# First FFN product: left operands begun three steps ahead instead of two, a ring of four, and weight blocks loaded in the order of use

## The chip, the cores and the metric

The kernel runs on one core of one Trainium2 chip. The core has five engines that work at the same time, each through its own list of instructions in the order in which the program issued them: TensorE (PE in the profile; PEld is its weight load), VectorE (DVE), ScalarE (ACT), GpSimd (POOL) and SyncE (SP), which here only issues transfers between DRAM and on-chip memory. An instruction that needs another engine's result or a transfer waits, and everything behind it in its list waits too. The metric is the device time of one execution in microseconds, lower is better.

## What is computed

An encoder trunk of two layers over x of 1024 tokens by 1024 features: layer 0 is a gated linear attention, layer 1 a chunked softmax attention, and each is followed by the same kind of convolutional FFN. The change lies in the FFN:

```python
D_MODEL = 1024; SEQ = 1024; DEPTH = 2; FFN_DIM = 2816; FFN_CONV = 3

def conv_ffn(xn, w_up, conv_w, conv_b, w_down):
    h = causal_dwconv(xn @ w_up, conv_w) + conv_b      # w_up: 1024 x 5632
    gate, val = h[..., :FFN_DIM], h[..., FFN_DIM:]
    return (jax.nn.silu(gate) * val) @ w_down          # w_down: 2816 x 1024

for layer in range(DEPTH):
    ...
    h = h + conv_ffn(rmsnorm(h, f_norm[layer]), f_w_up[layer], f_conv[layer], f_conv_b[layer], f_w_down[layer])
return rmsnorm(h, final_norm)
```

## The kernel before

**Precision.** Each float32 factor is cut in two numbers of the type fp32r, a high part (a copy on ACT, `cut_high`, L1370) and a low part (source minus high part, mostly on POOL, `cut_low`, L1375, shown in the profile under the helper's line L1355). A product is then three matmuls: high by high, high by low, low by high (`triple`, L1384 to L1386). In the profile the left operand of the first product is `uh` and `ul`, that of the second product `dh` and `dl`, and the raw weights behind them are `r` and `dr`.

**Columns and products.** The FFN's 5632 hidden columns are 22 column pairs j, each one block of 128 gate columns and one of 128 val columns. For one pair, the weights are four raw blocks (11, 12, 21, 22; upper and lower half of the features, gate and val), each loaded by SP with 256 KB (`load`, L1427). Column 0 takes eight plain products. For every other pair the 2 x 2 blocks are multiplied in the manner of Strassen and Winograd with seven products n, in the order 1, 7, 6, 5, 2, 4, 3. Each is one step of twelve matmuls of 512 columns, 2.7 us. The left operand of a product is built by `operand(j, n)` (L1433): for n = 7, 6, 5 and 3 a sum of raw blocks in place on DVE (`r<-r,r`), then the cast `uh` on ACT, then the subtraction `ul` on POOL. The first few products (those before (1, 3)) take the low part on DVE, and are begun two steps ahead. The right operands X are sums of the input halves, built once.

**After a product.** `after(j, n)` (L1495) runs in the step behind product n and adds the accumulator into `keep`, `vpre` or `gpre`. When a column's seven products are done, its conv runs: three taps of val and of gate (the first on ACT, L1464, two more on DVE, L1467), silu on ACT (L1470), the product with val on DVE, and the cut of the hidden block (`hidh` on ACT, L1482, `hidl` on DVE).

**The second product** (`down(g, u)`, L1660) runs in between: nine groups g of two columns, eight output tiles u = d0 to d7 each. From column 3 on, a period of two columns runs on PE as n3' d0 | n1 n7 d1 n6 d2 n5 n2 d3 n4 d4 n3 | n1' d5 n7' d6 n6' n5' d7 n2' n4' n3' d0, where n and n' are products of the odd and the even column; the first two groups of layer 0 and the first of layer 1 are woven in at other places. For even u the operand dr is loaded five steps ahead and cut two steps ahead of its use (dh on ACT, dl on POOL); it serves two tiles. The running sum of a tile over the groups lies in DRAM: `load_h` fetches it to one of two tiles `hr`, `down_sum` (L1684, the step behind the product) adds the new part on DVE (`hr<-pd,hr`) and SP writes it back.

**The order.** All of it is written out by hand. `seq` is the list of PE's steps, and `jobs` holds for each step what the other engines begin in it, with a rank. The loop issues the jobs of step i in the order of their ranks, those of the same rank in the order in which they were entered, and then the step itself:

```python
for i in range(len(seq) + 8):
    for _, f in sorted(jobs.pop(i, ()), key=lambda j_: j_[0]):
        f()
    if i < len(seq):
        seq[i]()
```

Ranks that matter: 0 for `after` and `down_sum`, 1 for the left operands of the first product and, entered later, for the cut of dr, about 2 for the conv, 3 for loads of weights, 5 for `load_h`. So in one step DVE sees first the sums of the step behind, then the `r` sums, then the conv. Tiles come from rings: a tag with `bufs` tiles, where a new tile waits until the oldest is free. `uh` and `ul` have rings of three, of which `tmp()` (L1792) lends tiles to the norm behind the FFN; r11, r21 and r22 have two tiles each, r12 one. `pos[j, s]` with s from 1 to 7 is the step of the s-th product of column j in the order above, so s = 2 is product 7 and s = 3 is product 6.

## Time and profile before

| | us |
|---|---|
| median of 3 runs | 2670.28 (2663.6 to 2670.86) |
| the profiled execution | 2677.71 |
| its span in the trace | 2676.0 |

The mean granted clock of PE in the profiled execution is 0.993 of full speed. In the rows of the profile a group reads: line, engine, operation, result<-sources, shape, count, then busy time and mean length of one in ns, then the idle time ahead of them on their engine and what ended it. In a timeline each row is start, length, engine, line, operation, and in brackets the idle time before it with what ended it. In the list of waits: who waited for whom, the total in us, how many times, and the longest. Matmul records overlap, so the distance between starts is their pace, not their length. The lines that carry the argument stand in the prediction.

### The profile page before, as it was taken

What the parts mean: (1) busy time and instruction counts of PE and PEld (TensorE: products, weight loads), DVE (VectorE), ACT (ScalarE), POOL (GpSimd) and SP (SyncE); (2) the same over time, 40 slices, a digit from 0 to 9 for tenths busy, and PEclk for the clock granted to TensorE, in tenths of its full rate; (3) what the DMA queues carried; (4) which work ended last, traced back from release to release, by engine and by line L of the source; (5) the groups of instructions that cost most, each with busy time, mean ns of one, the idle gap of its engine ahead of it and who ended that gap; (6) DMA issues with size and microseconds to landing.
All of it is one profiled execution on the core that took longest, in us unless ns stands there. A gap on an engine that the chain in (4) does not pass through costs nothing.

```text
span 2676.0 us, 40971 instructions
## 1 busy us (share of the span) xinstructions
PE 2577.5 (96%) x15013; PEld 2160.6 (81%) x15013; DVE 1656.1 (62%) x2968; ACT 1190.8 (44%) x2398; POOL 1136.6 (42%) x1202
## 2 busy tenths in 40 slices
PE   7999999999999999999999999998999999999998
PEld 5888788888777778888778888887777888888886
DVE  5756765554765556666775666666487565655667
ACT  5444546563443333333455555555354333333333
POOL 3655543346343343443435444434343343343441
PEclk9999999999999999999999999999999999999999
DMA  4534345456245555555531111114222555565554
GB/s 131 135 102 117 116 121 158 140 166 180 66 134 191 189 192 185 189 189 192 189 110 50 49 51 47 42 48 147 88 87 87 174 192 190 194 204 189 189 177 146
DMA packets 335065, 370.86 MB, mean 139 GB/s; under 512 B 34576, under 2 KB 256528, under 8 KB 334864
## 3 DMA queue, kind: packets, MB, share of 16 engines
q1 hardware_dynamic: 329328, 357.50, 42.3%
q10 hardware_dynamic: 4896, 8.65, 0.9%
q0 software_dynamic: 640, 2.10, 0.3%
q8 instruction: 118, 1.93, 0.3%
q14 instruction: 83, 0.68, 0.1%
HBM read 250.15 MB, written 118.03 MB: 138 GB/s over the span
## 4 chain that ended last, share of the span: by engine, by line
PE 56%; issue 13%; POOL 8%; DVE 7%; DMA 4%; ACT 1%; SPq 1%; POOLq 0%; DVEq 0%; ACTq 0%
PE pu L1386 6%; PE pu L1385 6%; PE pu L1384 6%; POOL ul L1355 5%; PE acc L120 4%; PE acc L121 4%; PE acc L122 4%; PE pd L1682 2%; PE pd L1681 2%; PE pd L1680 2%; PE acco L120 2%; PE acco L122 2%; PE acco L121 2%; PE ptp L1999 2%; DMA dr<-in_f_w_down_dram 2%
## 5 line engine op out<-in xcount | busy, mean ns | idle before, releaser
L1355 POOL TENSOR_TENSOR ul<-r,uh 128x512 fp32r<-128x512 f32 x282 | 402.3, 1435 | 669.4 <-ACT uh L1372 651.3
L1372 ACT CAST uh<-r 128x512 fp32r<-128x512 f32 x296 | 177.7, 618 | 536.8 <-DVE r L1355 499.9
L1355 DVE TENSOR_TENSOR hr<-pd,hr 128x1024 f32<-128x1024 f32 x136 | 166.4, 1223 | 352.9 <-DMA hr<-d_hu 192.7
L120 PE MATMUL acc<-xh,whi 128*128 128x512 f32 x896 | 375.8, 420 | 0.2 <-ACT xh L1094 0.2
L121 PE MATMUL acc<-xl,whi 128*128 128x512 f32 x896 | 354.4, 396 | 1.6 <-POOL xl L379 0.9
L122 PE MATMUL acc<-xh,wlo 128*128 128x512 f32 x896 | 353.3, 394 | 0.5 <-POOL wlo L105 0.5
L105 POOL TENSOR_TENSOR wlo<-wraw,whi 128x256 fp32r<-128x256 f32 (+1 forms) x293 | 235.9, 834 | 200.1 <-ACT whi L103 159.3
L1386 PE MATMUL pu<-xh,ul 128*128 128x512 f32 x552 | 217.4, 394 | 10.6 <-POOL ul L1355 10.4
L1384 PE MATMUL pu<-xh,uh 128*128 128x512 f32 x552 | 216.2, 392 | 1.7 <-DVE h L1256 0.9
L1385 PE MATMUL pu<-xl,uh 128*128 128x512 f32 x552 | 215.6, 391 | 1.0 <-POOL xl L379 1.0
L122 PEld LDWEIGHTS acc<-xh,wlo 128*128 128x128 f32 x896 | 169.3, 189 | 38.4 <-POOL wlo L105 1.0
L121 PEld LDWEIGHTS acc<-xl,whi 128*128 128x128 f32 x896 | 170.5, 190 | 25.9 <-POOL xl L379 3.1
L120 PEld LDWEIGHTS acc<-xh,whi 128*128 128x128 f32 x896 | 170.2, 190 | 23.2 <-ACT xh L1094 1.1
L1680 PE MATMUL pd<-dh,hidh 128*128 128x256 f32 x576 | 163.3, 284 | 0.0
L1682 PE MATMUL pd<-dh,hidl 128*128 128x256 f32 x576 | 163.0, 283 | 0.0
L1681 PE MATMUL pd<-dl,hidh 128*128 128x256 f32 x576 | 163.0, 283 | 0.0
L1467 DVE SCALAR_TENSOR_TENSOR val<-vpre,colt,val 128x1023 f32<-128x1023 f32 (+2 forms) x92 | 127.9, 1390 | 40.1 <-ACT val L1464 39.9
L1979 POOL TENSOR_SCALAR sS<-sS,st 128x640 f32<-128x640 f32 (+4 forms) x128 | 88.1, 691 | 144.9 <-DVE st L1978 121.4
L1355 POOL TENSOR_TENSOR dl<-dr,dh 128x512 fp32r<-128x512 f32 x72 | 98.7, 1371 | 105.8 <-ACT dh L1372 103.9
L1355 DVE TENSOR_TENSOR r<-r,r 128x512 f32<-128x512 f32 x168 | 136.2, 811 | 4.8 <-POOL ul L1355 4.7
L1386 PEld LDWEIGHTS pu<-xh,ul 128*128 128x128 f32 x552 | 103.6, 188 | 41.0 <-POOL ul L1355 19.6
L1977 ACT ACTIVATE sS<-sS,st 128x640 f32<-128x640 f32 (+4 forms) x128 | 89.2, 697 | 82.6 <-DVE st L1976 79.9
(374 smaller groups left out, 6738.2 us busy)
## 6 DMA issues: line engine op xcount, KB each, us to landing
d_hu<-hr SPq DMA_DIRECT2D x144, 512.0 KB, 3.0
hr<-d_hu SPq DMA_DIRECT2D x128, 512.0 KB, 5.0
r<-in_f_w_up_dram SPq DMA_DIRECT2D x168, 256.0 KB, 4.4
dr<-in_f_w_down_dram SPq DMA_DIRECT2D x72, 256.0 KB, 4.7
wraw<-in_a_w_in_dram SPq DMA_DIRECT2D x32, 512.0 KB, 4.6
wraw<-in_a_w_out_dram SPq DMA_DIRECT2D x16, 512.0 KB, 4.3
d_r<-h ACTq DMA_DIRECT2D x32, 256.0 KB, 4.0
wraw<-in_w_kv_dram SPq DMA_DIRECT2D x16, 512.0 KB, 4.0
```

What stands on the lines that cost most here:

```text
L105: nc.gpsimd.tensor_tensor(lo[:, c], raw[:, c], hi[:, c].bitcast(F32), op=ALU.subtract)
L120: mm(ps, hi[:, kw, wcol : wcol + P], rh[k][s], start=st, stop=False)
L121: mm(ps, hi[:, kw, wcol : wcol + P], rl[k][s], start=False, stop=False)
L122: mm(ps, lo[:, kw, wcol : wcol + P], rh[k][s], start=False, stop=sp)
L1355: tt = lambda eng, o, a, b, op: eng.tensor_tensor(o, a, b, op=op)
L1372: copy(hi, src)
L1384: mm(ps, w[0][:, cw], x[0], start=first, stop=False, skip_group_check=True)
L1385: mm(ps, w[0][:, cw], x[1], start=False, stop=False, skip_group_check=True)
L1386: mm(ps, w[1][:, cw], x[0], start=False, stop=last, skip_group_check=True)
L1680: mm(o_, hh, w_[0][:, c], start=i == 0 and g != u, stop=False, skip_group_check=True)
L1681: mm(o_, hh, w_[1][:, c], start=False, stop=False, skip_group_check=True)
L1682: mm(o_, hl, w_[0][:, c], start=False, stop=i == 1, skip_group_check=True)
```

## The change

Left operands from product (1, 3) on are issued three steps ahead of their product in place of two, at the same rank. The rings of `uh` and `ul` get a fourth tile, in both places where their size is given. The loads of the next column's blocks 11 and 21 change places, so that 11 (used by products 1, then 5) is asked for at product 7 of the column before and 21 (first used by product 7) at product 6. The cut of dr, the conv, the sums and the order of PE's steps are left as they are.

```diff
         def cut_high(src, ring, copy=nc.scalar.copy):
-            hi, lo = [wf.tile([P, HALF], F32R, name=ring + x, tag=ring + x, bufs=3 if ring == "u" else 2) for x in "hl"]
+            hi, lo = [wf.tile([P, HALF], F32R, name=ring + x, tag=ring + x, bufs=4 if ring == "u" else 2) for x in "hl"]
             copy(hi, src)
             return hi, lo
...
             else:
-                at(i - 2, lambda j=j, n=n: operand(j, n), 1)
+                at(i - 3, lambda j=j, n=n: operand(j, n), 1)
             if n != 2 or j > 2:
                 at(i + 1, lambda j=j, n=n: after(j, n), 0)
...
         for j in range(3, FP - 1):
-            for q, s in ((21, 2), (11, 3), (22, 4), (12, 7)):
+            for q, s in ((11, 2), (21, 3), (22, 4), (12, 7)):
                 at(pos[j, s], lambda j=j, q=q: load(j + 1, q), 3)
...
                 def tmp():
                     rooms.append(rooms.pop(0))
-                    return wf.tile([P, HALF], F32, name="nt", tag=rooms[-1], bufs=3)
+                    return wf.tile([P, HALF], F32, name="nt", tag=rooms[-1], bufs=4)
```

## The prediction

> **What bounds the kernel now.** I read the head of the page first, then the waits of TensorE (PE), over the span and stretch by stretch, then the timeline of each engine around single waits.

> ```profile
> span 2676.0 us, 40971 instructions
> PE 2577.5 (96%) x15013; PEld 2160.6 (81%) x15013; DVE 1656.1 (62%) x2968; ACT 1190.8 (44%) x2398; POOL 1136.6 (42%) x1202
> L1355 DVE TENSOR_TENSOR hr<-pd,hr 128x1024 f32<-128x1024 f32 x136 | 166.4, 1223 | 352.9 <-DMA hr<-d_hu 192.7
> ```

> PE is busy for 96% of the span and its matmuls stay the same in number and order. So the change can only shorten PE's waits in the two FFN stretches (some 680 to 1326 us and 1990 to 2626 us), or add to them. The third row is needed below: the running sum of the second product (hr) waits 192.7 us for its own reload from DRAM, and what stands behind such a sum in VectorE's (DVE's) order waits with it. The waits of PE, first the whole span, then 716 to 750, 750 to 875, 875 to 1300, 1300 to 1326, 2000 to 2040, 2135 to 2596 and 2596 to 2626 us (total, times, longest):

> ```profile
> PE pu L1386 <- POOL ul L1355: 19.6, 24, 1.7
> ...
> PE pu L1386 <- POOL ul L1355: 2.3, 2, 1.7
> PE pu L1384 <- DVE keep L1355: 1.1, 1, 1.1
> ...
> PE pu L1386 <- POOL ul L1355: 2.8, 4, 0.9
> PE pu L1384 <- ACT uh L1372: 1.2, 2, 0.9
> ...
> PE pu L1386 <- POOL ul L1355: 4.8, 7, 1.0
> ...
> PE pu L1384 <- ACT uh L1372: 0.4, 1, 0.4
> ...
> PE pu L1386 <- POOL ul L1355: 1.5, 2, 0.9
> ...
> PE pu L1386 <- POOL ul L1355: 2.3, 2, 1.7
> ...
> PE pu L1386 <- POOL ul L1355: 1.4, 2, 1.2
> ...
> PE pu L1386 <- POOL ul L1355: 1.8, 3, 0.8
> PE pu L1384 <- ACT uh L1372: 1.3, 1, 1.3
> ```

> These are the waits for the left operands, uh and ul. 16.9 of the first row's 19.6 us are found again in the stretches: that is what there is to win, about 1% with all that hangs on it. One such wait, on ScalarE (ACT), GpSimd (POOL) and PE:

> ```profile
> 1172.12 1.06 ACT L1470 ACTIVATE gate<-gate 128x1024 f32<-128x1024 f32 x1 [5.77 <-DVE gate L1467]
> 1173.09 1.12 ACT L1372 CAST uh<-r 128x512 fp32r<-128x512 f32 x2
> ...
> 1173.77 3.10 POOL L1355 TENSOR_TENSOR ul<-r,uh 128x512 fp32r<-128x512 f32 x2 [6.05 <-ACT uh L1372]
> ...
> 1174.31 0.39 PE L1385 MATMUL pu<-xl,uh 128*128 128x512 f32 x1
> 1175.67 0.50 PE L1386 MATMUL pu<-xh,ul 128*128 128x512 f32 x1 [0.97 <-POOL ul L1355]
> ```

> The cast of operand (j,2) stands behind silu on ACT, and silu had waited 5.77 us for DVE. A matmul starts 0.227 us after the one before it where nothing waits (two in 0.45 us, from 1224.35 to 1224.80 below). Here 1.36 us pass: 1.13 us are lost for a wait that reads 0.97, so each wait costs its figure plus 0.16.

> **What the change removes.** The cast and the low part go one step (2.7 us, twelve matmuls) earlier. In this example they come ahead of silu, and the wait goes. From 875 to 1300 us that saves 4.8 + 0.4 + 8 x 0.16 = 6.5 us, from 2135 to 2596 us 1.4 + 2 x 0.16 = 1.7 us: **-8.2**. At the end of layer 0 it is 1.5 + 0.3 = 1.8, of which I take -1.5. At the end of layer 1 it is 1.8 + 1.3 + 4 x 0.16 = 3.7 and one stretch at half clock:

> ```profile
> 2613.60:2617.00 3.40, 1.72 (x7) 0.78 (x5) 2.48 (x4) 2.09 (x3) 1.09 (x1) 1.00 0.02 5
> 2617.10:2620.40 3.30, 3.16 (x8) 2.49 (x9) 2.96 (x4) 0.25 (x1) 0.08 (x1) 0.50 0.27 79
> ...
> 737.00:740.40 3.40, 2.52 (x11) 2.13 (x12) 2.17 (x2) 1.45 (x3) 3.40 (x3) 1.00 0.26 106
> ```

> (Columns: stretch, its length, PE, PEld, DVE, ACT, POOL busy, granted clock, DMA share, GB/s.) In the first row PE is idle for 1.68 us of 3.40, and the next stretch runs at 0.50: 8 matmuls where 3.30 / 0.227 = 14.5 fit, so 1.5 to 1.7 us lost, 1.6 below. With 0.88 us idle (third row) no clock is lost. Of the 3.7 + 1.6 I take **-4** for the end of layer 1: other left operands there still queue with the last columns' cuts.

> [...]

> **What comes back.** Column 2's first saving, at 737 us, is not kept:

> ```profile
> 742.66 1.41 DVE L1355 TENSOR_TENSOR keep<-pu,keep 128x512 f32<-128x512 f32 x2
> ...
> 744.22 0.47 PE L1384 MATMUL pu<-xt4h,uh 128*128 128x512 f32 x1 [1.09 <-DVE keep L1355]
> ```

> Product (2,4) cannot start before that keep sum, which ends at 744.07 and is set by DVE's and ACT's conv work, not by PE. If (2,6) starts 1.9 us earlier, PE waits 1.9 us longer here; the same at this place of layer 1. Saving 0 (at best -1.9 in each layer). The two idles become one of almost 3 us in one stretch, which by the rows above costs the clock: **+1.6** in layer 0, while layer 1 pays for its own already.

> **What the change adds.** No work, and no DMA: the loads of blocks 11 and 21 change places (one 256 KB load each), the fourth tile of the ring takes room only; both 0, hidden by loads that lie more than a column ahead. The cost lies in the order. At lead 2 the operands of the second product (dr cast to dh on ACT, dl on POOL, two steps ahead) had a step to themselves. At lead 3 the steps before a down product also carry a left operand, emitted first. The worst place is once in two columns, around the fifth to seventh down product (d4 to d6). At lead 2, in group 7 (DVE, ACT, POOL, PE):

> ```profile
> 1215.46 1.23 DVE L1355 TENSOR_TENSOR hr<-pd,hr 128x1024 f32<-128x1024 f32 x1 [3.67 <-issue]
> 1216.60 1.28 DVE L1467 SCALAR_TENSOR_TENSOR val<-vpre,colt,val 128x1023 f32<-128x1023 f32 x1
> 1217.79 0.68 DVE L1355 TENSOR_TENSOR gpre<-pu,keep 128x512 f32<-128x512 f32 x1
> 1218.39 0.68 DVE L1355 TENSOR_TENSOR r<-r,r 128x512 f32<-128x512 f32 x1
> 1218.99 1.28 DVE L1467 SCALAR_TENSOR_TENSOR val<-vpre,colt,val 128x1022 f32<-128x1022 f32 x1
> ...
> 1212.27 1.24 ACT L1464 ACTIVATE val<-vpre,colt 128x1024 f32<-128x1024 f32 x1
> 1219.24 0.62 ACT L1372 CAST uh<-r 128x512 fp32r<-128x512 f32 x1 [5.73 <-PE pu L1386]
> ...
> 1222.07 1.28 POOL L1355 TENSOR_TENSOR dl<-dr,dh 128x512 fp32r<-128x512 f32 x1 [0.65 <-ACT dh L1372]
> 1225.26 1.61 POOL L1355 TENSOR_TENSOR ul<-r,uh 128x512 fp32r<-128x512 f32 x1 [1.91 <-ACT uh L1372]
> ...
> 1224.35 0.39 PE L1384 MATMUL pd<-hidh,dh 128*128 128x512 f32 x1
> 1224.80 0.39 PE L1386 MATMUL pd<-hidh,dl 128*128 128x512 f32 x1
> ```

> ACT's val (1212.27) ran while DVE waited for hr's reload, and dl of d6 was ready at 1223.35, 1.45 us before its use at 1224.80. After the change the order is: hr sum of d4, r of the next column's product 7, val taps, gpre, val taps, r of product 6; on ACT the cast for product 7 stands ahead of val; on POOL ul of product 6 stands ahead of dl of d6. One chain from the start of the hr sum: sum to r 1.14, r 0.68, hand-over 0.16, cast to val 0.52, val 1.24, hand-over 0.03, val taps 1.19, gpre 0.60, val taps 1.19, r 0.68, hand-over 0.03, cast 0.62, hand-over 0.08, ul 1.29 to 1.61 (middle 1.45), dl 1.28: **10.9 us** in all (start-to-start figures from the DVE rows). In group 7: 1215.46 + 10.9 = 1226.36, 1.56 us after 1224.80. So d6 waits where nothing waited before. The hr sum hangs on its reload and doesn't move. The same with the first of these groups (layer 0, group 2) and the last (layer 1, group 8), DVE and PE:

> ```profile
> 911.32 1.23 DVE L1355 TENSOR_TENSOR hr<-pd,hr 128x1024 f32<-128x1024 f32 x1 [3.71 <-DMA hr<-d_hu]
> ...
> 920.18 0.39 PE L1386 MATMUL pd<-hidh,dl 128*128 128x512 f32 x1
> ...
> 2570.92 1.22 DVE L1355 TENSOR_TENSOR hr<-pd,hr 128x1024 f32<-128x1024 f32 x1 [3.62 <-DMA hr<-d_hu]
> ...
> 2580.49 0.28 PE L1681 MATMUL pd<-dl,hidh 128*128 128x256 f32 x1
> ```

> 911.32 + 10.9 - 920.18 = 2.04 and 2570.92 + 10.9 - 2580.49 = 1.33. Done for all 15 such groups, seven in layer 0 give 11.2 and eight in layer 1 10.1: **+21.3** (from 15 with chains 0.4 shorter to 27 with 0.4 longer). Four of them are near 2 us; a wait of 1.9 falls with enough of itself into one 3.4 us stretch about every second time: **+3.2** for two half-clock stretches (0 to 24, if all 15 did). dl of d4 now stands behind product 3's operand, with 0 to 0.4 us to spare: **+1** (0 to 3). The two first groups of layer 0, woven otherwise, save 2.8 + 1.2 + 6 x 0.16 = 5.0 and, walked in the same way, get four new waits of 0.25 to 1.5 us, 4.1 in all: **-0.9** (-5 to +2).

> **Sum.** -8.2 - 1.5 - 4 + 1.6 + 21.3 + 3.2 + 1 - 0.9 = +12.5 us on the profiled execution of 2677.71 (1.7 of it outside the span). That execution lies 7.4 us above the median of the runs, 2670.28; the waits should be alike in both, so 2670.28 + 12.5 = 2683.

> **Rivals.** (B) Only the removal works: the chain of 10.9 us overlaps more than I allow, d6 keeps its 1.45 us, and the saving is 8.2 + 1.8 + 5.3 + 5.0, with some of column 2: -20 to -24, about 2648. For it: every wait in the second fence is one for a left operand. Against it: on DVE, ACT and POOL the new order leaves no branch of the chain free. (C) The trade evens out: hr reloads come 0.7 us earlier after the shortened waits, the new stalls halve to 10 or 11 us, and no clock is lost: 12.5 - 10.6 - 4.8 = -3, or +2 with the clock lost all the same: about 2670. For it: the sums wait for DMA, whose times scatter. [...] (D) The change doesn't do what it says: the earlier operand still stands behind the late hr sum, before's waits stay, and d6's come on top: 12.5 + 13 = +26, 2696. Against it: the casts that are now ahead of silu are freed whatever the sum does. (E) d6's wait costs the clock nearly each time, from the point where 1.7 us of idle fall into one stretch: 13 more stretches x 1.6 = 21 us more, 2704.

> **How the numbers follow.** Forecast 0.57, B 0.13, C 0.16, D 0.07, E 0.07. A difference of 0.3% (8 us) is about what can be told from none here. Faster: B and a tail of C, 0.15. Same: the rest of C and the forecast's lower end, 0.19. Slower: 0.66. The forecast alone reaches from 2674 to 2696 by its bounds. The range, 2660 to 2700, takes in C and D and leaves out B and most of E, 0.18.

> **What would show it.** Right: after the change PE waits at d6 for POOL's dl some 15 times, 1 to 2 us each; waits for ul from 875 to 1300 and 2135 to 2596 us are nearly gone; ACT's val follows uh directly behind an hr sum; (2,4) waits longer for keep. Wrong: no wait for dl, or waits for ul as before; then B or D holds.

## The result and the profile after

| | before | changed |
|---|---|---|
| median of the runs beside each other | 2669.23 us (4 runs, 2663.6 to 2670.86) | 2698.1 us (4 runs, 2696.57 to 2703.13) |
| profiled executions | 2677.71, later again 2668.14 | 2697.21 |
| their spans | 2676.0 and 2666.4 | 2695.1 |

The medians lie 28.9 us apart; the ratio, taken over all the runs and not from the two medians, is 1.0115, with a 95% interval of 1.0102 to 1.0128: the changed kernel is slower. The forecast was slower by 12.5 us. The direction was right, and so was the mechanism in the later groups of the second product. In the first two groups of layer 0 the forecast saw next to no cost, and there lies most of what is missing: 12.5 us are less than half of the real difference.

The head and two groups of the page of the changed kernel:

```profile
span 2695.1 us, 40987 instructions
...
PE 2579.4 (96%) x15013; PEld 2164.4 (80%) x15013; DVE 1683.3 (62%) x2968; ACT 1190.6 (44%) x2398; POOL 1136.4 (42%) x1202
...
L1355 DVE TENSOR_TENSOR hr<-pd,hr 128x1024 f32<-128x1024 f32 x136 | 166.5, 1224 | 266.2 <-DMA hr<-d_hu 126.1
```

PE, DVE, ACT and POOL have as many instructions as before. DVE's took 27 us longer in all (1683.3 for 1656.1); the gate taps grew most (L1467, 1633 ns each for 1303), and no experiment shows why. The changed kernel's waits of PE (who for whom, total in us, times, longest):

```profile
PE pd L1386 <- POOL dl L1355: 16.3, 12, 2.3
...
PE pd L1681 <- POOL dl L1355: 7.6, 7, 2.1
PE pu L1384 <- DVE keep L1355: 7.5, 2, 3.8
...
PE pu L1386 <- POOL ul L1355: 4.7, 5, 1.5
...
PE pd L1384 <- ACT dh L1372: 3.3, 2, 3.0
PE pu L1384 <- DVE vpre L1355: 3.0, 1, 3.0
```

The wait for ul, 19.6 us before (13.0 in the second trace of the same kernel, experiment 4), has shrunk to 4.7. In its place stand 23.9 us for dl (16.3 + 7.6) and 3.3 for dh, of which the kernel before had not one row. Cut to 750 to 875 us, then 875 to 1310, then 2145 to 2616 us, the lines for dh and dl are:

```profile
PE pd L1386 <- POOL dl L1355: 6.3, 4, 2.3
PE pd L1384 <- ACT dh L1372: 3.3, 2, 3.0
...
PE pd L1386 <- POOL dl L1355: 10.0, 8, 1.8
...
PE pd L1681 <- POOL dl L1355: 7.6, 7, 2.1
```

The last two rows are what was forecast for d6 and d4: 17.6 us in 15 waits (thirteen at d6, two short ones at d4), 20.0 with 0.16 for each, where the forecast had 21.3 and 1. The chain itself, in the same group 7 as in the prediction (DVE, ACT, POOL, PE):

```profile
1230.87 1.23 DVE L1355 TENSOR_TENSOR hr<-pd,hr 128x1024 f32<-128x1024 f32 x1 [3.40 <-DMA hr<-d_hu]
1232.01 0.68 DVE L1355 TENSOR_TENSOR r<-r,r 128x512 f32<-128x512 f32 x1
1234.57 1.28 DVE L1467 SCALAR_TENSOR_TENSOR val<-vpre,colt,val 128x1023 f32<-128x1023 f32 x1 [1.88 <-ACT val L1464]
...
1237.57 0.68 DVE L1355 TENSOR_TENSOR r<-r,r 128x512 f32<-128x512 f32 x1
...
1232.77 0.62 ACT L1372 CAST uh<-r 128x512 fp32r<-128x512 f32 x1 [7.98 <-issue]
1233.30 1.24 ACT L1464 ACTIVATE val<-vpre,colt 128x1024 f32<-128x1024 f32 x1
...
1238.29 0.62 ACT L1372 CAST uh<-r 128x512 fp32r<-128x512 f32 x1
...
1238.98 1.30 POOL L1355 TENSOR_TENSOR ul<-r,uh 128x512 fp32r<-128x512 f32 x1 [4.22 <-ACT uh L1372]
1240.23 1.72 POOL L1355 TENSOR_TENSOR dl<-dr,dh 128x512 fp32r<-128x512 f32 x1
...
1242.01 0.50 PE L1386 MATMUL pd<-hidh,dl 128*128 128x512 f32 x1 [1.21 <-POOL dl L1355]
```

Read it by its starts: the hr sum waits 3.40 us for its reload, r follows it, the cast follows r, val on ACT follows the cast (before, it had run during the sum's wait), and DVE's val taps now wait 1.88 us for ACT. From the start of the sum to the end of dl it is 1241.95 - 1230.87 = 11.1 us, where the prediction had added up 10.9.

**Where the time lies.** The time between the same two matmuls, counted in PE's order, in three traces (the cuts are named by the first trace's times; us):

| stretch | before, 1st | before, 2nd | changed | changed - 2nd |
|---|---|---|---|---|
| 0 to 680 (no FFN) | 680.55 | 682.15 | 677.88 | -4.3 |
| 680 to 716 (column 0) | 35.51 | 35.50 | 37.06 | +1.6 |
| 716 to 750 (columns 1, 2) | 33.95 | 34.23 | 36.46 | +2.2 |
| 750 to 876 (first two groups) | 126.19 | 126.42 | 137.86 | +11.4 |
| 876 to 1300 (the other groups) | 423.83 | 418.40 | 427.91 | +9.5 |
| 1300 to 1380 (end of layer 0) | 80.01 | 78.77 | 75.05 | -3.7 |
| 1380 to 1990 | 610.11 | 608.35 | 609.01 | +0.7 |
| 1990 to 2040 (layer 1, columns 1, 2) | 49.98 | 50.03 | 52.26 | +2.2 |
| 2040 to 2135 | 94.99 | 94.99 | 94.99 | 0 |
| 2135 to 2596 | 461.04 | 458.74 | 467.55 | +8.8 |
| 2596 to 2640 (end of layer 1) | 44.04 | 43.03 | 43.30 | +0.3 |
| rest | 35.82 | 35.83 | 35.82 | 0 |

The second trace of the kernel before is one of its usual executions, and its difference to the changed kernel's, 28.7 us, is nearly that of the medians. The +1.6 of column 0 is one stretch at half clock, from 680.22 us, which neither trace of before has there; the trace with the ring of four alone has one too (36.81 us for this row), that of experiment 1 has none (35.49). So this row varies from run to run. One row stands out that the prediction did not have: 750 to 876 us. There the rows of before and after read, first DVE and ACT of before (its first trace), then DVE, ACT and PE of the changed kernel:

```profile
771.03 1.23 DVE L1355 TENSOR_TENSOR hr<-pd,hr 128x1024 f32<-128x1024 f32 x1 [3.09 <-DMA hr<-d_r]
...
769.00 0.60 ACT L1372 CAST dh<-dr 128x512 fp32r<-128x512 f32 x1
```

```profile
773.00 1.23 DVE L1355 TENSOR_TENSOR hr<-pd,hr 128x1024 f32<-128x1024 f32 x1 [3.01 <-DMA hr<-d_r]
774.14 0.68 DVE L1355 TENSOR_TENSOR r<-r,r 128x512 f32<-128x512 f32 x1
...
774.90 0.62 ACT L1372 CAST uh<-r 128x512 fp32r<-128x512 f32 x1 [3.76 <-DVE r L1355]
775.43 0.61 ACT L1372 CAST dh<-dr 128x512 fp32r<-128x512 f32 x1
...
776.10 0.80 PE L1384 MATMUL pd<-hidh,dh 128*128 128x512 f32 x1 [3.00 <-ACT dh L1372]
778.37 0.80 PE L1386 MATMUL pd<-hidh,dl 128*128 128x512 f32 x1 [1.05 <-POOL dl L1355]
```

Before, dh was cast at 769.00, two us ahead of the late hr sum. Now it stands behind a cast that stands behind r that stands behind that sum, and PE, which needs dh for the first matmul, waits 3.00 us, then 1.05 more for dl. In all there are six such waits from 750 to 875 us, 9.6 us (the first two rows of the list by stretches above). Behind this idle, 2.31 of 3.40 us in the first row below, the granted clock falls to 0.56 and 0.50 (stretches of the changed kernel; the last columns are granted clock, DMA share, GB/s):

```profile
772.00:775.40 3.40, 1.09 (x5) 0.56 (x3) 2.40 (x3) 0.49 (x1) 0.00 (x0) 1.00 0.14 54
775.40:778.80 3.40, 1.65 (x3) 0.93 (x4) 1.85 (x2) 2.59 (x5) 3.20 (x3) 0.56 1.00 335
778.80:782.20 3.40, 3.40 (x9) 2.63 (x9) 1.20 (x2) 0.00 (x0) 1.73 (x1) 0.50 0.04 12
...
931.00:934.00 3.00, 1.98 (x6) 1.64 (x7) 2.06 (x1) 1.07 (x2) 3.00 (x2) 0.80 0.98 306
934.00:937.40 3.40, 3.40 (x12) 2.60 (x12) 1.34 (x2) 0.00 (x0) 1.42 (x2) 0.67 0.10 40
```

The last two rows are the one wait at d6, 1.8 us long (the longest from 875 to 1310 us), that cost clock as well: 0.80, then 0.67. From 750 to 876 us PE has three stretches of 3.41 us at a granted clock of 0.50 (from 775.80, 779.21 and 796.28 us), the second trace of before has one (from 822.23).

### The profile page after: what moved, and what is told of

Read it like the earlier page. It is cut to its first block, busy times and chain, and to the rows that moved or that the text cites. A ratio compares the mean times of both kernels' runs of the same rounds, so it can differ in the third digit from the quotient of the medians.

```text
span 2695.1 us, 40987 instructions
## 1 busy us (share of the span) xinstructions
PE 2579.4 (96%) x15013; PEld 2164.4 (80%) x15013; DVE 1683.3 (62%) x2968; ACT 1190.6 (44%) x2398; POOL 1136.4 (42%) x1202
## 4 chain that ended last, share of the span: by engine, by line
PE 36%; issue 27%; POOL 14%; DVE 9%; DMA 3%; ACT 2%; POOLq 0%; SPq 0%; DVEq 0%; ACTq 0%
POOL ul L1355 8%; PE acc L120 4%; PE acc L121 4%; PE acc L122 4%; POOL dl L1355 3%; PE acco L120 2%; PE acco L122 2%; PE acco L121 2%; PE pu L1384 2%; PE pu L1386 2%; PE pu L1385 2%; PE ptp L1999 2%; POOL wlo L105 1%; PE poT L2029 1%; PE poT L2028 1%
## 5 line engine op out<-in xcount | busy, mean ns | idle before, releaser
L1355 POOL TENSOR_TENSOR ul<-r,uh 128x512 fp32r<-128x512 f32 x282 | 404.6, 1439 | 794.2 <-ACT uh L1372 783.6
L1372 ACT CAST uh<-r 128x512 fp32r<-128x512 f32 x296 | 180.5, 617 | 451.9 <-DVE r L1355 265.1
L1355 DVE TENSOR_TENSOR hr<-pd,hr 128x1024 f32<-128x1024 f32 x136 | 166.5, 1224 | 266.2 <-DMA hr<-d_hu 126.1
L1384 PE MATMUL pu<-xh,uh 128*128 128x512 f32 x552 | 217.6, 394 | 4.5 <-DVE vpre L1355 3.0
L1386 PE MATMUL pu<-xh,ul 128*128 128x512 f32 x552 | 216.2, 392 | 2.8 <-POOL ul L1355 2.8
L1385 PE MATMUL pu<-xl,uh 128*128 128x512 f32 x552 | 216.6, 392 | 1.0 <-POOL xl L379 1.0
L1681 PE MATMUL pd<-dl,hidh 128*128 128x256 f32 x576 | 163.7, 284 | 7.6 <-POOL dl L1355 7.6
L1467 DVE SCALAR_TENSOR_TENSOR val<-vpre,colt,val 128x1023 f32<-128x1023 f32 (+2 forms) x92 | 115.6, 1256 | 77.9 <-ACT val L1464 77.8
L1467 DVE SCALAR_TENSOR_TENSOR gate<-gpre,colt,gate 128x1023 f32<-128x1023 f32 (+2 forms) x92 | 150.3, 1633 | 13.3 <-ACT gate L1464 13.1
L1355 DVE TENSOR_TENSOR r<-r,r 128x512 f32<-128x512 f32 x168 | 139.8, 832 | 2.6 <-POOL ul L1355 2.5
L1470 ACT ACTIVATE gate<-gate 128x1024 f32<-128x1024 f32 (+1 forms) x46 | 47.1, 1024 | 192.6 <-DVE gate L1467 192.6
L1386 PE MATMUL pd<-hidh,dl 128*128 128x512 f32 x288 | 116.0, 403 | 16.3 <-POOL dl L1355 16.3
```

The lines of the kernel that those rows point to most:

```text
L1355: tt = lambda eng, o, a, b, op: eng.tensor_tensor(o, a, b, op=op)
L1372: copy(hi, src)
L1384: mm(ps, w[0][:, cw], x[0], start=first, stop=False, skip_group_check=True)
L1385: mm(ps, w[0][:, cw], x[1], start=False, stop=False, skip_group_check=True)
L1386: mm(ps, w[1][:, cw], x[0], start=False, stop=last, skip_group_check=True)
L1467: nc.vector.scalar_tensor_tensor(t_[:, a:c1], p_[:, a - step : c1 - step], w[:, 2 - step : 3 - step], t_[:, a:c1], op0=ALU.mult, op1=ALU.add)
```

## The experiments

All times are medians; the ratio, taken over all runs, is to the kernel before, run beside each on the same chip. Four questions: is it the order of dl and ul; what do the first two groups cost; do the ring and the loads count; and does the left operand cost by its place ahead of dl or by the late sum it hangs on.

**1. The cut of dr ahead of the left operand.** In the changed kernel:

```diff
-  at(i - 2, lambda g=g, u=u: dops.__setitem__((g, u), cut(draw[g, u], "d")), 1)
+  at(i - 2, lambda g=g, u=u: dops.__setitem__((g, u), cut(draw[g, u], "d")), 0.9)
```

> The changed kernel, but the cut of dr (dh on ACT, dl on POOL) is issued ahead of the left operand of the same step instead of behind it. Theory (the new waits are dh and dl queued behind a left operand that hangs on a late hr sum): the 23 waits of PE for dl and dh (27.2 us) are gone but for a few, and with the half-clock stretches behind them the time falls by 28 to 33 us from 2698 to 2665-2670, about the time before. Rival 1 (the left operand, now behind dl, is late in its place): ul waits of 1.3 us come back about once in two columns, 2675-2690. Rival 2 (the waits come from late loads of dr or from lead 3 itself): no change, 2698.

Measured: 2671.01 us (10 runs), ratio 1.0009 (0.9998 to 1.0019). One digit of a rank takes back 27 of the 28.9 us. Its waits of PE:

```profile
PE pu L1384 <- DVE keep L1355: 9.6, 4, 3.8
PE pu L1386 <- POOL ul L1355: 5.1, 6, 1.5
PE pu L1384 <- DVE vpre L1355: 3.0, 1, 3.0
...
PE pd L1386 <- POOL dl L1355: 1.2, 2, 0.6
```

27.2 us for dh and dl have become less than 2, and the waits for ul did not come back. The stretch from 750 to 876 us falls from 137.86 to 123.82 us. The first theory holds and both rivals fall. (One us of its expected 2665 to 2670 is missed.) What is left is no profit: the kernel with lead 3 and without its harm is as fast as the one before.

**2. Lead 2 for columns 3 to 6 of layer 0.** In the changed kernel:

```diff
-  at(i - 3, lambda j=j, n=n: operand(j, n), 1)
+  at(i - (2 if layer == 0 and 3 <= j < 7 else 3), lambda j=j, n=n: operand(j, n), 1)
```

> The changed kernel, but in columns 3 to 6 of layer 0 (its first two groups of the second product) the left operands are begun two steps ahead as before. Theory (these columns lost 16.4 us in the changed kernel and 4.9 in the one before, which the prediction took as about nothing): the time falls by 10 to 13 us to 2685-2688, and the waits at d6 of the later groups stay, 17 to 18 us. Rival (the stalls of these columns come from the bigger ring or the swapped loads): no change, 2698.

Measured: 2689.67 us (4 runs), ratio 1.0073 (1.0057 to 1.0089). 8.4 us are won (7.4 by the distance of the medians to the kernel before, 11 by the ratios), where 10 to 13 were expected. In the trace the stretch from 750 to 876 falls from 137.86 to 123.25 us, 14.6 less, and its waits for dh and dl are gone. The next stretch, 876 to 1300, is 6.0 us longer than in the changed kernel (433.94 to 427.91). Its waits for dl are 11.6 us in place of 10.0, and 23 matmuls there run at half pace (0.427 us from start to start in the changed kernel's eight, against 0.227) in place of 8, 0.2 us each, together some 4.6 of the 6.0. So the term of the first two groups is confirmed. The 15 matmuls more at half pace are two half-clock stretches more: three waits of 1.79 us at d6 are each followed by one, where the changed kernel has one such place. Whether that is chance or comes with the edit, one trace doesn't tell; the last section has two such waits of the changed kernel, one with a half-clock stretch behind it and one without.

**3 and 4. The ring of four alone, and the kernel before once more.** The first is the kernel before with both `bufs=3` changed to 4.

> The kernel before with the ring of four alone; lead and loads as before. Theory (the ring only makes room): the same as before within 3 us, 2667-2672, and the waits for ul stay at 19 to 20 us. Rival (a cast at lead 2 waits for the ring of three, as one row of the kernel before seems to say): some of the ul waits go, up to 10 us faster.

> The kernel before, unchanged, for a second profile. Its first profile, 2677.7 us, was 8.5 us above the median of its runs, the changed kernel's was at its median. If that profile was an outlier, this one is at 2664-2671, and the rows that differ from the first tell where the 8 us are. If profiling costs this kernel that much, it is again near 2677.

Measured: 2668.69 us (10 runs), ratio 1.0002 (0.999 to 1.0014) for the ring: no effect. The unchanged kernel's second profile took 2668.14 us, so the first, 2677.71, was an outlier of this kernel (of its 85 other runs one was longer). The waits for ul and uh in the second one, and then in the one with the ring of four:

```profile
PE pu L1386 <- POOL ul L1355: 13.0, 16, 1.7
PE pu L1384 <- ACT uh L1372: 2.7, 3, 1.3
```

```profile
PE pu L1386 <- POOL ul L1355: 14.0, 18, 1.7
PE pu L1384 <- ACT uh L1372: 4.1, 6, 1.6
```

13.0 us in 16 waits stand where the first profile had 19.6 in 24. The 14.0 of the ring is therefore no gain, and the expected 19 to 20 us were the outlier's. From 876 to 1300 and 2135 to 2596 us the outlier is 5.4 and 2.3 us longer than the second trace (table above), just where the prediction had put its largest saving.

**5. Lead 3 for columns 3 to 20 alone**, with the cut of dr first as in 1:

```diff
+  at(i - (3 if 3 <= j < FP - 1 else 2), lambda j=j, n=n: operand(j, n), 1)
```

> As in the run with the cut of dr issued first, and columns 1, 2 and 21 keep lead 2 (lead 3 for columns 3 to 20 alone). Theory: lead 3 in columns 1 and 2 cost 2.3 us in each layer (the keep wait of product (2,4) becomes one idle of 3.8 us with a half-clock stretch behind it) and about 1.3 us at the end of layer 1 (vpre); without them 2671 falls by 5 to 6 us to 2664-2667, 1 to 4 us less than the kernel before (2668.2): the whole profit of lead 3. Rival (lead 3 in the middle saves nothing that chance doesn't): 2668-2671, the same as before.

Measured: 2670.85 us (12 runs), ratio 1.0014 (1.0004 to 1.0024). My expectation falls, the rival holds. Lead 2 in the first and last columns wins nothing; with it product (2,6) waits for ul again, and product (2,4) still waits 2.0 us for keep. Columns 1 and 2 of layer 0 take 36.43 us, as with lead 3 (36.49 in experiment 1), not 34.23. The trace shows where the difference lies: the half-clock stretch comes behind the keep wait here (from 747.14 us), while the second trace of before has it ahead of the keep sum (from 740.30), where it fills time that PE would have waited.

**6. Product 6 alone at lead 2** (columns 3 to 21) in the changed kernel, so that no ul stands ahead of dl of d6:

```diff
+  at(i - (2 if n == 6 and j > 2 else 3), lambda j=j, n=n: operand(j, n), 1)
```

> The changed kernel with product 6 alone back at two steps in columns 3 to 21, so that dl of d6 has no ul ahead of it on POOL that hangs on the late sum. Theory of the chain of 10.9 us: its last links (second val taps, r, cast and ul of product 6) fall away, dl of d6 needs some 9.2 us from the hr sum and is due after 9.3 or more in most groups, so the waits for dl from 875 us on (17 to 18 us) shrink to 0-4 us, and the time falls by 13 to 18 us to 2680-2685; the waits of the first two groups of layer 0 stay for the most part. Rival (it is the place of product 7's r behind the hr sum alone that makes dl late): the waits stay above 10 us, 2692-2698.

Measured: 2681.59 us (4 runs, 2676.53 to 2688.94; the trace is of the fastest), ratio 1.0052 (1.0033 to 1.0071), as expected. The waits for dl from 875 to 1310 and from 2135 to 2600 us:

```profile
PE pd L1386 <- POOL dl L1355: 0.6, 2, 0.4
...
PE pd L1681 <- POOL dl L1355: 0.2, 1, 0.2
```

0.8 us in place of 17.6, while r of product 7 still stands behind the hr sum. So without the last links of the chain (second val taps, r, cast and ul of product 6) the earlier ones are not enough to make dl late in most groups. 3.9 us of waits for ul, six, come in their place between 875 and 1310 us. In the first two groups 4.1 us for dl and 3.3 for dh remain, which product 6 does not explain.

**7. The swapped loads alone, and 8. experiment 1 with the loads as before.**

> The kernel before with the loads of blocks 11 and 21 in the new order alone. Theory (loads lie more than a column ahead of their use): the same as before within 3 us, 2665-2671, no wait for a load of raw weights. Rival (a later load of 21 meets the traffic of hr and makes sums late): slower by 5 us or more.

> The changed kernel with the cut of dr issued first, and the loads of blocks 11 and 21 in the order of before. If the 0.13% of the run with the swapped loads alone is real, this one is 3 to 4 us faster than the 2671.0 with the cut first: 2666-2668, no different from the kernel before. If it was scatter: 2670-2672.

Measured: 2672.51 us (10 runs), ratio 1.0013 (1.0001 to 1.0024), and 2670.95 us (11 runs), ratio 1.0002 (0.9993 to 1.0012). The first is 1.5 us above what was expected. The second is no different from experiment 1 (2671.01), which has the new order. PE waits for a load of raw weights in no trace, and POOL's waits for r are the same with the swap alone (5.6 and 4.6 us) as in the second trace of before. The interval of the first barely leaves 1; 8 speaks for scatter. If the swap costs anything, it is not seen beside lead 3.

**9. The left operand ahead of the hr sum.** In the changed kernel, with the cut of dr still behind it:

```diff
-  at(i - 3, lambda j=j, n=n: operand(j, n), 1)
+  at(i - 3, lambda j=j, n=n: operand(j, n), -0.5)
```

> The changed kernel, but each left operand is issued at the start of its step (rank -0.5), ahead of the hr sum and of what follows product by product; the cut of dr stays behind it. Theory (the left operand in front of dl costs only because it hangs on the hr sum that waits for its reload): r of product 7 no longer stands behind the sum, the chain from the hr sum to dl of d6 shrinks by 1.14 + 0.68 + 0.52 + 0.16 to some 8.5 us, shorter than the 9.3 to 9.8 us there are, so the waits for dl from 875 us on (17 to 18 us) shrink to 0-3 us, and the waits for dh and dl in the first two groups too: 2668-2676. Rival (POOL's and ACT's work in front of dl is what counts, whatever it waits for): waits of over 10 us stay, 2688-2698. Second rival (the sums that free accumulators are now later by 0.7 to 1.8 us): waits for vpre or keep of 1 us and more in many columns, 2680 and up.

Measured: 2663.52 us (9 runs), ratio 0.9976 (0.9964 to 0.9988), 4.5 us better than the expected range. The waits for dl from 750 to 875 and from 875 to 1310 us:

```profile
PE pd L1386 <- POOL dl L1355: 1.0, 2, 0.8
...
PE pd L1386 <- POOL dl L1355: 0.2, 1, 0.2
```

The left operand is still issued ahead of dl. It does no harm there once it no longer hangs on the sum that waits for its reload. The second rival shows a little: keep waits of 12.2 us over the whole span (7.5 in the changed kernel).

**10, 12. Both first, with the loads as before**, run twice:

```diff
+  at(i - 3, lambda j=j, n=n: operand(j, n), -0.5)
...
+  at(i - 2, lambda g=g, u=u: dops.__setitem__((g, u), cut(draw[g, u], "d")), -0.6)
```

> As the run before it, the cut of dr ahead of the left operand as well, and the loads in the order of before. Theory: no left operand hangs on an hr sum and no cut of dr on a left operand; what is left of the waits are those of columns 1, 2 and 21 (some 10 us with their half-clock stretches): 2660-2667, at best 8 us less than the kernel before. Rival (the sums are late instead): 2670 and up.

> The run with both first once more, beside the one at lead 2 on the same chip: again 2658-2664, 0.2 to 0.4% less than the kernel before.

Measured: 2660.43 us (5 runs), ratio 0.9969 (0.9956 to 0.9981), and again 2660.3 us (9 runs), ratio 0.9969 (0.9957 to 0.998). This beats both kernels. The timeline of group 7 (DVE, ACT, POOL, PE) shows why:

```profile
1200.19 0.68 DVE L1355 TENSOR_TENSOR r<-r,r 128x512 f32<-128x512 f32 x1
1203.58 1.23 DVE L1355 TENSOR_TENSOR hr<-pd,hr 128x1024 f32<-128x1024 f32 x1 [2.70 <-issue]
...
1201.48 1.24 ACT L1464 ACTIVATE val<-vpre,colt 128x1024 f32<-128x1024 f32 x1
...
1208.52 1.74 POOL L1355 TENSOR_TENSOR dl<-dr,dh 128x512 fp32r<-128x512 f32 x1 [5.57 <-ACT dh L1372]
...
1213.44 0.39 PE L1386 MATMUL pd<-hidh,dl 128*128 128x512 f32 x1
```

r is done before the hr sum waits, val runs on ACT during that wait as it did in the kernel before, and dl is ready at 1210.26, 3.2 us ahead of its use. With the cut of dr in front, what dh still waits for is its own load: ACT waits 17 times for dr, 14.9 us in all and 2.6 at most, and PE waits for dl nowhere. From 750 to 876 us this kernel needs 120.35 us (126.42 in the second trace of before), from 876 to 1300 us 414.31 (418.40). It gives some of that back in columns 1 and 2, where the keep wait of (2,4) is 4.35 us (36.94 and 52.54 us, against 34.23 and 50.03).

**11. The kernel before with the left operands first**, at lead 2 and with its ring of three:

```diff
-  at(i - 2, lambda j=j, n=n: operand(j, n), 1)
+  at(i - 2, lambda j=j, n=n: operand(j, n), -0.5)
```

> The kernel before (lead 2, ring of three, loads as they were), only with the left operands issued at the start of their step (rank -0.5), ahead of the hr sum. If it is the place ahead of the hr sum that pays, and not the third step, it is as fast as the run with both first (2660-2664). If the third step is needed too (casts behind silu, a ring of three that makes a cast wait for PE), the ul and uh waits stay for the most part (over 8 us) and it is at 2665-2669.

Measured: 2671.13 us (12 runs), ratio 1.0011 (1.0 to 1.0022), 2 us above the expected 2665 to 2669. Its waits for operands:

```profile
PE pu L1386 <- POOL ul L1355: 12.8, 20, 1.5
PE pu L1384 <- DVE keep L1355: 6.6, 2, 3.3
PE pu L1384 <- ACT uh L1372: 2.8, 4, 1.6
```

The waits for ul stay. The place ahead of the sum alone pays nothing, and lead 3 behind the sum, with its harm to dl taken out (experiment 1), pays nothing; the two together are worth 6 us (experiment 9) to 8 us (10 and 12). Lead 2 in this place with a ring of four was not run, so a share of the ring in this gain isn't ruled out; at the old place it had no effect (experiment 3).

## Why the prediction was right in kind and wrong in size

- **The chain of 10.9 us at d6: right.** 11.1 us in the group shown, waits in thirteen of the fifteen groups, 20.0 us with d4's and their restarts against 21.3 + 1 forecast. Experiments 1, 6 and 9 each break the chain at another link, and each time these waits go but for 0.2 to 1.4 us.
- **"The two first groups of layer 0 ... -0.9": the step that failed.** 12.3 of the 16.2 us that the sum was short lie here (+11.4 measured). The prediction walked these groups with the later groups' pattern, ul ahead of dl, at 0.25 to 1.5 us each. Here it is also dh, behind a left operand's cast, behind r, behind an hr sum that waits for d_r: 3.00 us at once, for the first matmul of the tile, with more for dl and half-clock stretches behind it. In place of four new waits of 4.1 us there were six of 9.6, and two half-clock stretches more than in the second trace of before, for which this step had no term. The bound of +2 was no bound. Experiments 1 and 2 take 14.0 and 14.6 us out of this stretch.
- **The saving of 8.2 us between the columns: over-sized.** Priced with 0.16 per wait, the second trace has 2.2 + 0.4 us in 5 waits from 875 to 1310 us and none for a left operand from 2135 to 2590: 3.4 us. The rows were read rightly but came from an execution 9.6 us longer than the next one, and "the waits should be alike in both" was the wrong assumption. In the sum this is nearly made up for by d6 waits 2.3 us and clock 1.6 us below the forecast (its two half-clock stretches at d6 were an estimate from two rows; the trace has one, from 932.81 us): +18.3 measured (9.5 + 8.8), +17.3 forecast.
- **Column 2: right that nothing is won, too low in cost.** Forecast +1.6 in layer 0 and 0 in layer 1, measured +2.2 in each; the keep wait is 3.76 and 3.75 us, and the half-clock stretch now comes behind it (from 745.08 and 2045.55 us) and adds to it. "Layer 1 pays for its own already" was wrong: both traces of before have that stretch ahead of the keep sum (in the first from 2026.54 us, the sum from 2030.71), and there one cost 0.3 us in layer 0 (34.23 against 33.95).
- **The end of layer 1: -4 forecast, +0.3 measured.** The waits for uh and ul of before are gone, but product (21,3) waits 3.03 us for vpre, which DVE reaches late. "Take -4" left out that the vpre sum there is late, behind conv work (val by gate, 2.28 us) and a cut for the last product on DVE. And the half-clock stretch that was to go is there again (from 2639.47 us); experiment 2's trace, with the same vpre wait and no such stretch, takes 41.78 us in place of 43.30. At the end of layer 0, -1.5 forecast, -3.7 measured; part of that is luck, since both traces of before have a half-clock stretch in this row and the changed kernel's has none.
- **Ring and loads at 0: held**, by experiments 3 and 8; the interval of 7 leaves room for 0.1%.
- The stretches outside these (0 to 716 and 1380 to 1990) differ by -2.0 together, which no step of the prediction explains. The differences from the forecast add up: 12.3 (first two groups) + 2.8 (column 2) + 1.0 (the later groups) + 4.3 and - 2.2 (ends of layer 1 and 0) - 2.0 = 16.2, and 12.5 + 16.2 = 28.7.
- **Rivals.** Not C: no stall halved, though the sums' waits for DMA do scatter (1.28 to 6.13 us each in the first trace of before). Not B, not D: the ul waits did go. E's extra clock loss came, but in the first two groups and hardly at d6, where one of thirteen waits cost a stretch (three of them in experiment 2's trace).

## What to carry to other kernels

Starting an operand earlier was not free here although its engines were far from full (DVE busy for 62% of the span, ACT 44%, POOL 42%): it moved in front of something else in their lists and brought along what it waits for itself, so that dh stood behind a left operand's cast and PE waited 3.00 us for it. Before moving a step, look for what it hangs on (here a sum that waits for a transfer) and for who is now behind it; put the work that hangs on nothing first, then the earlier start pays (-8 us here, +29 without). And take the waits of a tuned kernel from two executions, since a third of them can be one execution's own (here 6.6 of 19.6 us for ul).

## What the runs showed of the hardware that was not expected

A half-clock stretch was nearly free in one place. In columns 1 and 2 of layer 0 the first trace of before lost no clock and waited 1.09 us for keep. The second ran matmuls at half pace (from 740.30 us) right after the same 1.9 us stall and then had no keep wait: 33.95 and 34.23 us for the same work. Ahead of the keep sum the slower clock only filled the wait; behind the keep wait it came on top: 36.46 us in the changed kernel and 36.43 in experiment 5.
